# Tying the order of TensorE through a dilated attention mixer, and of VectorE's weight sums ahead of it

## The chip, the cores and the metric

The kernel runs on one core of a Trainium2 chip. The metric is the device time of one execution in microseconds (us); the kernel before has a median of 1405.3 us over three runs (1405.26 to 1405.36). In what follows PE is TensorE, DVE is VectorE, ACT is ScalarE, POOL is GpSimd and SP is SyncE.

## The reference, cut to what matters

A two-layer encoder over 512 tokens of width 1024, all in float32. Each layer is a token mixer and a squared-ReLU MLP, each with a norm ahead and a residual sum behind. The change lies in the first mixer, dilated attention with three head groups g, whose outputs are merged by their softmax denominators:

```python
qkv = (h @ w_qkv).reshape(B, S, 3, N_GROUPS, A_HEADS, A_HEAD_DIM)
for g, (window, dil) in enumerate(((128, 1), (512, 4), (2048, 16))):
    q = rope(rms_norm(qkv[:, :, 0, g], q_gain[g]), S)
    k = rope(rms_norm(qkv[:, :, 1, g], k_gain[g]), S)
    v = qkv[:, :, 2, g]
    o, lse = dilated_group(q, k, v, window, dil)   # softmax over |i-j| <= window/2, every dil-th key
    ...
wts = softmax(stack(lses, 0), axis=0)
o = sum(wts[g][..., None] * outs[g] for g in range(3))
return o.reshape(B, S, 1024) @ w_o
```

There are 8 heads of 128. The second layer's mixer is a latent attention (mixer B); the change does not touch it, nor the MLPs.

## The kernel before, in words

Each float32 product of the large matrices is made of three matmuls on halves: weights are loaded as `raw` (SP's queue), ACT copies the rounded upper part to `whi` (L158), DVE subtracts it for the lower part `wlo` (L159), and PE adds `whi` x upper, `wlo` x upper and `whi` x lower of the activations (L191). `whi` and `wlo` have rings of 4 buffers, `raw` of 3.

The stages follow each other: the **V phase** makes the values v of all groups, mainly by a scheme with seven block products for eight (function `v_phase`, products at L436, each group's blocks `b11` to `b22` and their sums `bT` and `b3` by `add_block`, L349; DVE splits the weights at L422 and adds or subtracts finished products into `vo` at L455). Then **mixer A**, then MLP, **mixer B** and MLP.

Mixer A goes over four head pairs b and three groups g: twelve projection blocks `(b, g)`, each `block_groups` (L163) with four out tiles r of 128 tokens by 512 columns and four weight units u, loaded in two groups of two. So a block has 16 steps `(r, u)`, each of 6 matmuls: steps 0 to 7 take units 0 and 1 for r = 0 to 3, steps 8 to 15 units 2 and 3. The four out tiles take the four PSUM banks of `acc_p`. `qk_evac` empties a bank: ACT squares it (L138, four times), DVE multiplies it with the rotary tables (L288, and L291 twice), makes `rs_v` (L130), POOL raises it to -1/2, DVE adds and scales (L296, L297), ACT rearranges halves (L299), SP's queue transposes by DMA and ACT writes `qkT` (L307).

`scores` (L591, L595 for g = 0, L602 for g = 1 and 2) multiplies q with k into a bank of `sc_p` (two banks), DVE adds a mask, takes a maximum (L598, L607, L610), ACT takes exponentials (L613). `merge` combines the three groups' maxima and denominators through two small matmuls (`scm`, L657 and L682) and DVE scales the probabilities P (L688). `pv` transposes P on PE into a bank of `tp_p` (two banks; L125), copies it (`pT`, on DVE at L698 for groups 1 and 2, on ACT at L705 for group 0) and adds up four heads' products into `sco` (L712, L716), which DVE copies to `oT` (L718). `split_o` (L761, L762) halves `oT` for the out projection `a_w_o`; `v_last` is the value projection of the eighth head, 4 tiles of 384 columns.

[...] The code can add an order of its own: `tc.issue_after(x)` holds what is issued inside behind the instruction x, and (new in the change) `tc.keep_in_program_order` keeps an engine's instructions in the order of the code. In the kernel before, PE's order through mixer A is the scheduler's.

Of the kernel before, what the change touches and what calls it, by code (L numbers as in the profile page):

```python
# [10 lines left out]
F32 = mybir.dt.float32  # L11
# [77 lines left out]
def encoder_kernel(ctx: ExitStack, tc: tile.TileContext, x, norm_mix, norm_ffn, a_w_qkv, a_q_gain, a_k_gain,  # L89
# [33 lines left out]

    def transpose(o, i):
        return PE.transpose(o, i, ident)  # L125
# [36 lines left out]
    def block_groups(units, groups, n, mm, outs=NT, halves=1, raws=None, order=None, between={}, by_k=False):  # L162
# [4 lines left out]
        kt0 = 0  # L167
        for gi, g in enumerate(groups):
# [9 lines left out]
            if by_k and gi == len(groups) - 1:  # L178
                steps = [(*step[:3], [j]) for j in range(loaded[0][2]) for step in steps]
            left = {o: sum(step[1] == o for step in steps) for o in range(outs)}  # L180
            cut = None
            for i, (hv, o, u, js) in enumerate(steps):
                hi, lo, nk = loaded[u]
                with ExitStack() as behind:
                    if cut is not None:
                        behind.enter_context(tc.issue_after(cut))
                        cut = None
                    for j in js:
                        kt = first[u] + j
                        for p_i, (lt, rt, oc) in enumerate(mm(o, kt, hi[:, j], lo[:, j], hv)):  # L190
                            last = PE.matmul(accs[o][:, oc], lhsT=lt, rhs=rt, start=(kt == 0 and p_i == 0 and hv == 0),  # L191
                                             stop=(kt == total - 1 and p_i == 2), skip_group_check=halves > 1)
                if i in between:
                    with tc.issue_after(last.ins):
                        cut = between[i]()
                left[o] -= 1
                if gi == len(groups) - 1 and not left[o]:
                    yield o, accs[o]
            if gi < len(groups) - 1:
                yield None  # L200
# [109 lines left out]
    def qk_proj(b, g, qkT, homes, junk, turned, midway):  # L310

        for end in block_groups(qk_units(b, g), [2, 2], 512, act_stationary(hT, 512)):
            if end is None:
                midway()
            else:
                qk_evac(g, qkT, *end, homes, junk, turned)()

# [4 lines left out]
    def v_phase(vp):  # L322
# [23 lines left out]
        def add_block(t, x, y):  # L346
            for u in range(2):
                us = slice(2 * u, 2 * u + 2)
                V.tensor_tensor(t[:, us], x[:, us], y[:, us], op=ALU.add)  # L349
# [68 lines left out]
        def split_w(x):  # L418
# [3 lines left out]
            V.tensor_tensor(lo, x, hi.bitcast(F32), op=ALU.subtract)  # L422
# [16 lines left out]
        def both(p, w, banks, first):  # L439
            for u, t in ((0, 0), (0, 1), (1, 0), (1, 1)):  # L440
# [21 lines left out]
        def piece(g, ba):  # L462
# [4 lines left out]
            add_block(bT[g], bT[g], b22[g])  # L467
# [66 lines left out]
        for g in range(1, NG):  # L534
# [7 lines left out]
            both(2, b21[g], bd, True)  # L542
            put(g, 0, 0, "set", bd, False)
# [15 lines left out]
    with tc.tile_pool(name="apool", bufs=1, reuse_waits="tile") as ap_, \  # L559
# [19 lines left out]
        def scores(b, g, qkT, Pt, stats):  # L579

            m, den, nb = stats
            for h in range(2):
                qT, kT = qkT[:, h], qkT[:, 2 + h]
                for part in range(2 if g == 0 else 1):
                    sc = sc_p.tile([P, 512], F32, tag="sc", name=nm("sc"))
                    pt = Pt[g][h]
                    if g == 0:
                        for ii in range(2):
                            i = 2 * part + ii
                            q_i = qT[:, i * P:(i + 1) * P]  # L590
                            PE.matmul(sc[:, ii * 256:ii * 256 + 128], lhsT=q_i, rhs=kT[:, i * P:(i + 1) * P],  # L591
                                      start=True, stop=True)
                            segs = bass.AP(tensor=kT.tensor, offset=kT.offset + SEG_A[i],
                                           ap=[list(kT.ap[0]), [SEG_B[i] - SEG_A[i], 2], [1, 64]])
                            PE.matmul(sc[:, ii * 256 + 128:ii * 256 + 256], lhsT=q_i, rhs=segs, start=True, stop=True)  # L595
                        sv = sc.rearrange("p (i k) -> p i k", i=2)
                        pv = pt[:, 2 * part:2 * part + 2, :]
                        V.tensor_tensor(pv, sv, m0[:, 2 * part:2 * part + 2, :], op=ALU.add)  # L598
                        cols = range(2 * part, 2 * part + 2)
                    else:  # L600
                        for r in range(NT):
                            PE.matmul(sc[:, r * P:(r + 1) * P], lhsT=qT[:, r * P:(r + 1) * P],  # L602
                                      rhs=kT[:, r * P:(r + 1) * P], start=True, stop=True)
                        sv = sc.rearrange("p (i k) -> p i k", i=NT)
                        pv = pt
                        mk = (m1 if g == 1 else m2).unsqueeze(1).broadcast_to([P, NT, P])
                        V.tensor_tensor(pv, sv, mk, op=ALU.add)  # L607
                        cols = range(NT)
                    c0, c1 = cols[0], cols[-1] + 1
                    V.tensor_reduce(m[:, g, h, c0:c1], pv, axis=AX.X, op=ALU.max)  # L610
                    V.tensor_scalar(nb[:, g, h, c0:c1], m[:, g, h, c0:c1], -SCALE_A, None, op0=ALU.mult)
                    for c in cols:
                        A.activation(pt[:, c], pt[:, c], AF.Exp, bias=nb[:, g, h, c:c + 1], scale=SCALE_A,  # L613
                                     accum_out=den[:, g, h, c:c + 1])
# [8 lines left out]
        def v_last(vt, v0n, v0c):  # L623
# [7 lines left out]
            run_block(v_units(HA - 1), [1] * 4, 384, act_stationary(hT, 384), evac)  # L631
# [15 lines left out]
        def merge(stats, Pt):  # L647

            m, den, _ = stats
# [6 lines left out]
            for s_ in range(4):  # L656
                PE.matmul(ps[:, 4 * s_:4 * s_ + 4], lhsT=xs[:, s_], rhs=r4, start=True, stop=True)  # L657
# [22 lines left out]
            ps2 = sc_p.tile([P, 512], F32, tag="sc", name=nm("scm"))  # L680
            for h in range(2):
                PE.matmul(ps2[:, 4 * h:4 * h + 4], lhsT=xs2[:, h], rhs=i4, start=True, stop=True)  # L682
            V.tensor_copy(e[:, 0], ps2[:, 0:8])
            ev = e.rearrange("p g (h i) -> p g h i", h=2)
            for h in range(2):
                for g in (1, 2, 0):
                    t = Pt[g][h]
                    V.tensor_tensor(t, t, ev[:, g, h].unsqueeze(2).broadcast_to(list(t.shape)), op=ALU.mult)  # L688

        def pv(b, h, Pt, vt, v0n, v0c):  # L690
            pts = []
            hs = slice(DH * h, DH * h + DH)
            for g in (1, 2):
                tp = tp_p.tile([P, 512], F32, tag="tp", name=nm("tp"))
                for r in range(NT):
                    transpose(tp[:, r * P:(r + 1) * P], Pt[g][h][:, r])
                pT = aw.tile([P, 512], F32, tag="pT", name=nm("pT"), bufs=4)
                V.tensor_copy(pT, tp)  # L698
                pts.append(pT)
            for part in range(2):  # L700
                tp = tp_p.tile([P, 512], F32, tag="tp", name=nm("tp"))
                for i in range(NT):
                    transpose(tp[:, i * P:(i + 1) * P], Pt[0][h][:, i, part * P:(part + 1) * P])
                pT = aw.tile([P, 512], F32, tag="pT", name=nm("pT"), bufs=4)
                A.activation(pT.rearrange("p (i r j) -> p i r j", i=NT, r=NT),  # L705
                             tp.rearrange("p (i j r) -> p i r j", i=NT, r=NT), AF.Copy)
                pts.append(pT)
            o = sc_p.tile([P, 512], F32, tag="sc", name=nm("sco"))
            ov = o.rearrange("p (r m) -> p r m", r=NT)
            for r in range(NT):  # L710
                for g in (1, 2):
                    PE.matmul(o[:, r * P:(r + 1) * P], lhsT=vt[:, r, g - 1, hs], rhs=pts[g - 1][:, r * P:(r + 1) * P],  # L712
                              start=(r == 0 and g == 1), stop=False, skip_group_check=True)
            for i in range(NT):
                for part, vv in ((0, v0n), (1, v0c)):
                    PE.matmul(ov[:, :, 32 * i:32 * i + 32], lhsT=vv[:, i, hs], rhs=pts[2 + part][:, i * P:(i + 1) * P],  # L716
                              start=False, stop=(i == NT - 1 and part == 1), skip_group_check=True)
            V.tensor_copy(oT[:, 2 * b + h], o)  # L718
# [10 lines left out]
        def project_in(b, g, midway=lambda: None):  # L729
            if b == 0 and g:  # L730
                tables(g, gqk[:, g - 1], ca[:, 0:256], ca[:, 256:768])
            qkT = aw.tile([P, 4, S], F32, tag="qkT", name=nm("qkT"))
            qk_proj(b, g, qkT, homes, junk, turned, midway)
            return qkT

        def finish(b, Pt, stats, vs):
            merge(stats, Pt)
            for h in range(2):
# [520 lines left out]
```

## Time and profile before

| | us |
|---|---|
| median of three runs | 1405.3 |
| profiled execution | 1403.76 |
| span of its trace | 1402.0 |
| PE busy | 1371.6 (98%) |
| DVE busy | 940.0 (67%) |
| ACT busy | 801.0 (57%) |
| POOL busy | 224.0 (16%) |

The stages lie about so in the span: V phase to 122 us, mixer A from there to 510, MLP to 830, mixer B to 1040, out projection and MLP to the end. A row of a list of groups gives line, engine, operation, output and inputs, the shape, the count, busy time and mean in ns, and the idle time ahead of it with what ended it. A row of waits gives the engine's line, what ended the wait, the total, the count and the longest. A timeline row gives start, duration, engine, line and operands, and in brackets the idle time ahead. A matmul's end is modelled, so its pace is read from two starts.

### The profile page before, as it was taken

To read this page: it belongs to the slowest core of one execution; us is meant where nothing else is said; L and a number is where in the kernel's file an instruction comes from. 1 tells how busy PE (TensorE), PEld (TensorE's weight loads), DVE (VectorE), ACT (ScalarE), POOL (GpSimd) and SP (SyncE) were. 2 spreads that over 40 slices of the span, in tenths; PEclk is the share of its full clock that TensorE was granted. 3 is DMA by queue.
4 is the path that set the end of the run, shared out by engine and by line. 5 is a ranking of instruction groups with operands and counts; after the bars stand their busy time and mean duration, and the time that the engine had idled before them with its cause. 6 is when DMAs were issued, how large, how long until landed. Compare 5 with 4: busy or idle time off the path is not lost.

```text
span 1402.0 us, 18979 instructions
## 1 busy us (share of the span) xinstructions
PE 1371.6 (98%) x6852; PEld 1163.6 (83%) x6852; DVE 940.0 (67%) x1498; ACT 801.0 (57%) x1643; POOL 224.0 (16%) x240
## 2 busy tenths in 40 slices
PE   7999999999999999999999999999999999999998
PEld 6999887888889989888888878777769888888887
DVE  6886777787788744464655768788745465574747
ACT  6544778687786624453536455777534553644543
POOL 1110212121122001020200204433201020020101
PEclk9999999999999999999999999999999999999999
DMA  9535553655555539486583944211116668493835
GB/s 309 170 134 163 134 130 97 164 131 125 143 130 120 158 106 271 135 186 174 123 237 87 234 96 95 61 31 31 46 46 189 172 131 230 98 234 119 198 88 120
DMA packets 171774, 197.83 MB, mean 141 GB/s; under 512 B 59104, under 2 KB 109024, under 8 KB 171680
## 3 DMA queue, kind: packets, MB, share of 16 engines
q1 hardware_dynamic: 152496, 157.55, 37.7%
q0 software_dynamic: 19184, 39.07, 15.5%
q8 instruction: 54, 0.88, 0.3%
q14 instruction: 40, 0.33, 0.1%
HBM read 176.13 MB, written 7.86 MB: 131 GB/s over the span
## 4 chain that ended last, share of the span: by engine, by line
PE 80%; DVE 7%; DMA 4%; issue 4%; ACT 3%; POOL 1%; SPq 0%; ACTq 0%; DVEq 0%; POOLq 0%
PE acc L191 49%; PE sc L877 9%; PE tp L877 6%; PE sc L436 3%; PE tp L125 2%; DMA wqs<-in_ffn_w_dram 2%; PE acc L1170 1%; DVE wlo L820 1%; PE sc L1064 1%; DMA xT<-t 1%; PE acc L1146 1%; PE tp L436 1%; PE sc L602 1%; PE sco L716 1%; PE sco L712 1%
## 5 line engine op out<-in xcount | busy, mean ns | idle before, releaser
L191 PE MATMUL acc<-whi,hT 128*128 128x512 f32 (+2 forms) x1208 | 377.2, 388 | 1.9 <-ACT hT L761 1.0
L191 PE MATMUL acc<-hT_f,whi 128*128 128x512 f32 (+1 forms) x1152 | 317.5, 366 | 0.0
L159 DVE TENSOR_TENSOR wlo<-raw,whi 128x1024 fp32r<-128x1024 f32 (+3 forms) x146 | 172.8, 1188 | 169.3 <-ACT whi L158 168.8
L191 PEld LDWEIGHTS acc<-whi,hT 128*128 128x128 f32 x1208 | 224.4, 188 | 42.7 <-ACT hT L761 1.7
L158 ACT ACTIVATE whi<-raw 128x1024 fp32r<-128x1024 f32 (+3 forms) x146 | 149.7, 1029 | 159.6 <-PE acc L191 74.8
L191 PEld LDWEIGHTS acc<-hT_f,whi 128*128 128x128 f32 x1152 | 207.9, 189 | 34.9
L191 PE MATMUL acc<-wlo,hT 128*128 128x512 f32 (+2 forms) x604 | 232.9, 386 | 0.4 <-DVE wlo L159 0.4
L820 DVE TENSOR_TENSOR wlo<-wqs,whi 128x1024 fp32r<-128x1024 f32 x112 | 137.7, 1231 | 114.0 <-ACT whi L819 113.9
L819 ACT ACTIVATE whi<-wqs 128x1024 fp32r<-128x1024 f32 x112 | 118.3, 1060 | 162.0 <-PE acc L191 66.2
L191 PE MATMUL acc<-hT_f,wlo 128*128 128x512 f32 (+1 forms) x576 | 204.1, 366 | 0.0
L877 PE MATMUL sc<-whi,asp 128*128 128x512 f32 x512 | 165.1, 390 | 1.0 <-DVE resid L851 1.0
L805 POOL DMA_DIRECT2D wqs<-in_ffn_w_dram x64 | 77.7, 1347 | 539.7 <-DVE wlo L820 358.1
L191 PEld LDWEIGHTS acc<-wlo,hT 128*128 128x128 f32 x604 | 113.7, 188 | 20.1 <-DVE wlo L159 1.0
L191 PEld LDWEIGHTS acc<-hT_f,wlo 128*128 128x128 f32 x576 | 108.3, 189 | 17.3
L877 PEld LDWEIGHTS sc<-whi,asp 128*128 128x128 f32 x512 | 96.2, 188 | 21.6 <-issue 1.8
L877 PE MATMUL tp<-whi,asp 128*128 128x512 f32 x352 | 112.1, 390 | 0.9 <-DVE resid L851 0.9
L133 POOL TENSOR_TENSOR qrs<-rs_v,nhalf 128x4 f32<-128x4 f32 x48 | 64.6, 1348 | 265.0 <-DVE rs_v L130 241.8
L877 PE MATMUL sc<-wlo,asp 128*128 128x512 f32 x256 | 99.7, 390 | 0.0
L307 ACT ACTIVATE qkT<-xT 128x1024 uint16<-128x1024 uint16 x48 | 56.5, 1181 | 39.5 <-DMA xT<-t 39.4
L877 PEld LDWEIGHTS tp<-whi,asp 128*128 128x128 f32 x352 | 66.1, 188 | 15.0 <-DVE resid L851 1.3
L877 PE MATMUL tp<-wlo,asp 128*128 128x512 f32 x176 | 68.2, 390 | 0.0
L138 ACT ACTIVATE junk<-acc 128x128 f32<-128x128 f32 x192 | 52.3, 273 | 12.3 <-PE acc L191 8.7
(236 smaller groups left out, 2186.8 us busy)
## 6 DMA issues: line engine op xcount, KB each, us to landing
wqs<-in_ffn_w_dram SPq DMA_DIRECT2D x80, 512.0 KB, 5.0
raw<-in_ffn_w_dram SPq DMA_DIRECT2D x64, 512.0 KB, 4.6
wqs<-in_ffn_w_dram POOLq DMA_DIRECT2D x64, 512.0 KB, 7.2
raw<-in_a_w_qkv_dram SPq DMA_DIRECT2D x96, 256.0 KB, 3.2
b<-in_a_w_qkv_dram SPq DMA_DIRECT2D x24, 384.0 KB, 5.7
vall<-vo POOLq DMA_DIRECT2D x24, 192.0 KB, 2.3
raw<-in_a_w_o_dram SPq DMA_DIRECT2D x8, 512.0 KB, 4.1
raw<-in_b_w_o_dram SPq DMA_DIRECT2D x8, 512.0 KB, 3.8
```

The source lines that it names most:

```text
L125: return PE.transpose(o, i, ident)
L133: G.tensor_tensor(out, v[:, :n], nhalf[:, :n], op=ALU.pow)
L138: A.activation(junk, x, AF.Square, scale=1.0 / math.sqrt(dim), accum_out=out)
L158: A.activation(hi[:, :nk, :n], raw[:, :nk, :n], AF.Copy)
L159: V.tensor_tensor(lo[:, :nk, :n], raw[:, :nk, :n], hi[:, :nk, :n].bitcast(F32), op=ALU.subtract)
L191: last = PE.matmul(accs[o][:, oc], lhsT=lt, rhs=rt, start=(kt == 0 and p_i == 0 and hv == 0), stop=(kt == total - 1 and p_i == 2), skip_gr ...
L307: A.activation(dst, xT.rearrange("p (h c) t -> p c t h", h=2), AF.Copy)
L436: PE.matmul(banks[t][:, :VH], lhsT=lt, rhs=rt[:, j], start=(first and k == 0 and i_ == 0), stop=(k == 3 and i_ == 2), skip_group_check=True)
L805: marks["sum"] = nc.gpsimd.dma_start(t, src, accum_op=ALU.add).ins
L819: A.activation(hi, x, AF.Copy)
L820: V.tensor_tensor(lo, x, hi.bitcast(F32), op=ALU.subtract)
L877: PE.matmul(bk[t], lhsT=lt, rhs=rt[:, j], start=(first and k == 0 and i_ == 0), stop=(k == 3 and i_ == 2), skip_group_check=True)
```

## The change

Three things are new.

**PE's order through mixer A is tied.** While `tied[0]` holds, every matmul and transpose of PE keeps the order of the code. The code is written so that a projection block runs step by step, whole steps of six matmuls, and the pieces of attention have places behind numbered steps (`sides`): the score parts of the head pair, the merge in two parts (`fold`: first the small matmuls and the scaling of groups 1 and 2, then the second small matmuls and the scaling of group 0), and the four parts of `pv` for each head (transposes of groups 1 and 2, their products, transposes of group 0, their products). The attention of pair c runs in the blocks of pair c+1; that of the last pair runs between the steps of `v_last` and of the first half of the out projection, which now runs in half steps (one k tile after the other over its four out tiles) and lies wholly in the tied stretch.

**DVE's sums in the V phase are tied later.** For groups 1 and 2 the sum `bT` = `b11` + `b12` stands behind the last product subtracted for the group before (`marks["minus"]`) and behind the split of product 2; the sum `b3` stands behind the sum `bT` + `b22`. Products 6 and 7 of these groups finish one out tile before the other. The rotary tables of group 0 move from group 1 to the end of the phase.

**The helpers are split up** so that each piece can be called by itself; what they compute is the same.

On DVE in the V phase, between group 1 (`bT_671`) and group 2 (`bT_949` before, `bT_945` now): in the order before,

```order
L422 TENSOR_TENSOR wlo_866<-b_110_824,whi_865 128x2x384
L349 TENSOR_TENSOR bT_949<-b_124_940,b_125_943 128x768 x2
L422 TENSOR_TENSOR wlo_882<-b_110_824,whi_881 128x2x384
L422 TENSOR_TENSOR wlo_902<-bT_671,whi_901 128x2x384
L455 TENSOR_TENSOR vo<-vo,sc_674 128x384
L349 TENSOR_TENSOR b_150_1098<-b_125_943,b_126_946 128x768
L455 TENSOR_TENSOR vo<-vo,sc_675 128x384
L349 TENSOR_TENSOR b_150_1098<-b_125_943,b_126_946 128x768
L422 TENSOR_TENSOR wlo_918<-bT_671,whi_917 128x2x384
L455 TENSOR_TENSOR vo<-vo,sc_674 128x384
```

and now

```order
L436 TENSOR_TENSOR wlo_862<-b_110_820,whi_861 128x2x384
L436 TENSOR_TENSOR wlo_872<-b_110_820,whi_871 128x2x384
L436 TENSOR_TENSOR wlo_898<-bT_671,whi_897 128x2x384
L469 TENSOR_TENSOR vo<-vo,sc_674 128x384
L469 TENSOR_TENSOR vo<-vo,sc_675 128x384
L436 TENSOR_TENSOR wlo_914<-bT_671,whi_913 128x2x384
L469 TENSOR_TENSOR vo<-vo,sc_674 128x384
L436 TENSOR_TENSOR wlo_951<-b_123_933,whi_950 128x2x384
L469 TENSOR_TENSOR vo<-vo,sc_675 128x384
L436 TENSOR_TENSOR wlo_967<-b_123_933,whi_966 128x2x384
L362 TENSOR_TENSOR bT_945<-b_124_936,b_125_939 128x768 x2
```

The sum for group 2 and the two halves of `b_150` (its `b3`) stood among the splits and vo rows of group 1; the sum now stands behind the last of these vo rows.

On DVE at the second part of a merge (here the second head pair's, whose place is in block (2,1)), where `me` is the weight of group 0, `P` 128x1024 a scaling of group 0, and `pT` the copies of the first head's transposes: before,

```order
L683 COPY me_3090<-scm_3103 128x8
L698 COPY pT_3118<-tp_3113 128x512
L159 TENSOR_TENSOR wlo_3521<-raw_3517,whi_3520 128x1024
L698 COPY pT_3125<-tp_3120 128x512
L297 TENSOR_TENSOR t_601_3367<-t_601_3367,qrs_3374 128x512
L296 TENSOR_TENSOR t_608_3400<-t_608_3400,t_609_3401 128x512
L688 TENSOR_TENSOR P_2329<-P_2329,me_3090 128x1024
L688 TENSOR_TENSOR P_2330<-P_2330,me_3090 128x1024
```

and now

```order
L711 COPY me_3132<-scm_3233 128x8
L308 TENSOR_TENSOR t_566_3206<-t_566_3206,t_567_3207 128x512
L669 TENSOR_TENSOR P_2620<-P_2620,me_3132 128x1024
L669 TENSOR_TENSOR P_2667<-P_2667,me_3132 128x1024
L727 COPY pT_3244<-tp_3239 128x512
L300 TENSOR_TENSOR t_578_3259<-acc_3080,cosg_1228 128x512
L727 COPY pT_3251<-tp_3246 128x512
```

The two copies stood ahead of the scalings of group 0 and now stand behind them. The third pair's rows read the same; in the first pair one copy stands right behind `me`, the other behind the scalings.

On DVE at the end of the projections, where `acc_4385` before and `acc_4242` now are the last out tile of block (3,2), whose bank the fourth tile of `v_last` takes next: before,

```order
L598 TENSOR_TENSOR P_4081<-sc_4114,ca 128x512
L610 TENSOR_REDUCE stat_4087<-P_4081 128x2
L288 TENSOR_TENSOR t_848_4579<-acc_4385,cosg_1230 128x512
L291 TENSOR_TENSOR t_849_4580<-acc_4385,sing_1231 128x4x64 x2
L130 TENSOR_SCALAR rs_v_4584<-qss_4573 128x4
```

and now

```order
L625 TENSOR_TENSOR P_4607<-sc_4606,ca 128x512
L300 TENSOR_TENSOR t_844_4564<-acc_4242,cosg_1230 128x512
L138 TENSOR_SCALAR rs_v_4569<-qss_4558 128x4
L308 TENSOR_TENSOR t_835_4518<-t_835_4518,t_836_4519 128x512
L628 TENSOR_REDUCE stat_4368<-P_4607 128x4
L303 TENSOR_TENSOR t_845_4565<-acc_4242,sing_1231 128x4x64 x2
```

The pair L291 (now L303), the bank's last reader, stood right behind the first reader and now stands behind `rs_v`, another tile's sum and a reduction. On PE the fourth tile of `v_last` starts one score and three steps behind the end of block (3,2); before, the scheduler ran three tiles of `v_last` with a first, one with a second weight unit and some scores ahead of the fourth tile.

The core of the diff:

```diff
+    def on_pe(ins):
+        return tc.keep_in_program_order(ins) if tied[0] else ins
+
+    def multiply(out, **kw):
+        return on_pe(PE.matmul(out, **kw))
...
-            if by_k and gi == len(groups) - 1:
+            if by_k == "all":
+                steps = [(0, o, u, [j]) for u in range(g) for j in range(loaded[u][2]) for o in range(outs)]
+            elif by_k and gi == len(groups) - 1:
...
-                if i in between:
+                if at + i in between:
                     with tc.issue_after(last.ins):
-                        cut = between[i]()
+                        cut = between[at + i]()
...
-        def both(p, w, banks, first):
-            for u, t in ((0, 0), (0, 1), (1, 0), (1, 1)):
+        def both(p, w, banks, first, by_tile=False):
+            for u, t in ((0, 0), (1, 0), (0, 1), (1, 1)) if by_tile else ((0, 0), (0, 1), (1, 0), (1, 1)):
...
             b3 = vp.tile([P, 4, VH], F32, tag="h32", name=nm("b3"))
-            add_block(b3, b12[g], b22[g])
-            both(6, bT[g], ba, False)
+            with ExitStack() as behind:
+                if g:
+                    behind.enter_context(tc.issue_after(after_t))
+                add_block(b3, b12[g], b22[g])
+            both(6, bT[g], ba, False, g > 0)
             put(g, 0, 1, "sub", ba, True)
-            add_block(bT[g], bT[g], b21[g])
-            both(7, b3, ba, False)
+            marks["sums", g] = add_block(bT[g], bT[g], b21[g])
+            both(7, b3, ba, False, g > 0)
             put(g, 1, 1, "sub", ba, True)
+            marks["minus", g] = marks["put"]
...
-            if g == 1:
-
-                with tc.issue_after(marks["put"]):
-                    tables(0, g0, rot[:, 0:256], rot[:, 256:768])
-            add_block(bT[g], b11[g], b12[g])
+            with tc.issue_after(marks["minus", g - 1]), tc.issue_after(seconds):
+                add_block(bT[g], b11[g], b12[g])
             piece(g, ba)
+        with tc.issue_after(marks["sums", NG - 1]):
+            tables(0, g0, rot[:, 0:256], rot[:, 256:768])
...
+        def fold(b, i):
+            if i == 0:
+                folds[b] = merge(stats[b], Pt[b])
+                return
+            folds[b]()
+            pvs[b] = [pv(b, h, Pt[b], *vs[b]) for h in range(2)]
...
+        def sides(b, g):
+
+            if b == 0:
+                return [{}, {13: at((score, 0, 0, 0)), 15: at((score, 0, 0, 1))},
+                        {1: at((score, 0, 0, 2)), 3: at((score, 0, 0, 3)), 14: at((score, 0, 1, 0))}][g]
+            c = b - 1
+            return [{0: at((score, c, 1, 1)), 13: at((score, c, 2, 0)), 15: at((score, c, 2, 1))},
+                    {3: at((fold, c, 0)), 11: at((fold, c, 1), (part, c, 0, 0)), 13: at((part, c, 0, 1)),
+                     14: at((part, c, 0, 2))},
+                    {0: at((part, c, 0, 3)), 1: at((part, c, 1, 0)), 3: at((part, c, 1, 2)), 4: at((part, c, 1, 1)),
+                     5: at((part, c, 1, 3)), 6: at((score, b, 0, 0)), 7: at((score, b, 0, 1)),
+                     8: at((score, b, 0, 2), (score, b, 0, 3)), 14: at((score, b, 1, 0))}][g]
+
+        tied[0] = True
         for b in range(HA // 2):
...
-        merge(stats, Pt)
-        v_last(*vs)
+        c = HA // 2 - 1
+        v_last(*vs[c], {1: at((score, c, 1, 1)), 12: at((score, c, 2, 0)), 13: at((score, c, 2, 1)),
+                        15: at((fold, c, 0))})
...
-        pv(HA // 2 - 1, 0, Pt, *vs)
-        first_cols = block_groups(w_units(a_w_o[0], 0, 512), [3, 1], 512, act_stationary(oA, 512, {0: o0}), by_k=True)
-        next(first_cols)
-        pv(HA // 2 - 1, 1, Pt, *vs)
-        for h in (HA - 2, HA - 1):
-            split_o(h)
+        first_cols = block_groups(w_units(a_w_o[0], 0, 512), [3, 1], 512, act_stationary(oA, 512, {0: o0}), by_k="all",
+                                  between={12: at((fold, c, 1), (part, c, 0, 0)), 15: at((part, c, 0, 1)),
+                                           17: at((part, c, 0, 2)), 19: at((part, c, 1, 0)),
+                                           20: at((part, c, 0, 3), (split_o, HA - 2)),
+                                           22: at((part, c, 1, 1), (part, c, 1, 2)),
+                                           24: at((part, c, 1, 3), (split_o, HA - 1))})
+        first_cols = iter([*first_cols])
+        tied[0] = False
```

`part(c, h, i)` calls the i-th of the four pieces of `pv` for head h of pair c: 0 turns groups 1 and 2 (`turn_strided`), 1 adds their products (`add_strided`), 2 turns group 0 (`turn_near`), 3 adds its products (`add_near`).

More of the change, by code (lines that the diff above doesn't have):

```diff
@@ L308, in qk_evac, with qk_proj @@
         return end
[L310 to L315, printed above, removed]
+    def qk_proj(b, g, home, homes, junk, turned, between):
+        qkT = None
+        for end in block_groups(qk_units(b, g), [2, 2], 512, act_stationary(hT, 512), between=between):
+            if end is not None:
+                qkT = qkT or home()
                 qk_evac(g, qkT, *end, homes, junk, turned)()
+        return qkT
     def load_gains(g, gqk):
@@ L348, in add_block @@
                 us = slice(2 * u, 2 * u + 2)
[L349 removed]
+                last = V.tensor_tensor(t[:, us], x[:, us], y[:, us], op=ALU.add)
+            return last.ins
         def load_x(r):
@@ L577, in encoder_kernel, with scores @@
         sel, r4, sel2, i4 = cc(C_SEL, C_R4), cc(C_R4, C_SEL2), cc(C_SEL2, C_I4), cc(C_I4, C_ALL)
-        def scores(b, g, qkT, Pt, stats):
+        def scores(g, h, part, qkT, Pt, stats):
             m, den, nb = stats
[L582 to L614, printed above, removed]
@@ L679, in merge, with rest @@
                                 sel2.unsqueeze(2).broadcast_to([P, 32, NT]), op=ALU.mult)
[L680 to L683, printed above, removed]
             ev = e.rearrange("p g (h i) -> p g h i", h=2)
             for h in range(2):
-                for g in (1, 2, 0):
-                    t = Pt[g][h]
-                    V.tensor_tensor(t, t, ev[:, g, h].unsqueeze(2).broadcast_to(list(t.shape)), op=ALU.mult)
+                for g in (1, 2):
+                    scale(g, h)
+            def rest():
+                ps2 = sc_p.tile([P, 512], F32, tag="sc", name=nm("scm"))
+                for h in range(2):
+                    multiply(ps2[:, 4 * h:4 * h + 4], lhsT=xs2[:, h], rhs=i4, start=True, stop=True)
+                V.tensor_copy(e[:, 0], ps2[:, 0:8])
+                for h in range(2):
+                    scale(0, h)
+            return rest
         def pv(b, h, Pt, vt, v0n, v0c):
@@ L708, in pv @@
[L708 to L717, printed above, removed]
@@ new lines, in add_near @@
+            def add_near():
+                ov = o[0].rearrange("p (r m) -> p r m", r=NT)
+                for i in range(NT):
+                    for part, vv in ((0, v0n), (1, v0c)):
+                        multiply(ov[:, :, 32 * i:32 * i + 32], lhsT=vv[:, i, hs],
+                                 rhs=pts[2 + part][:, i * P:(i + 1) * P],
+                                 start=False, stop=(i == NT - 1 and part == 1), skip_group_check=True)
+                V.tensor_copy(oT[:, 2 * b + h], o[0])
@@ L727, in turned, with project_in @@
             return aw.tile([P, 8, P], U16, tag="xT", name=nm("xT"))
-        def project_in(b, g, midway=lambda: None):
+        qk, Pt, stats, vs, folds, pvs = {}, {}, {}, {}, {}, {}
+        def project_in(b, g, between):
             if b == 0 and g:
                 tables(g, gqk[:, g - 1], ca[:, 0:256], ca[:, 256:768])
[L732 to L736, printed above, removed]
-            merge(stats, Pt)
-            for h in range(2):
-                pv(b, h, Pt, *vs)
@@ L742, in encoder_kernel, with score @@
-        qkT = project_in(0, 0)
+            qk[b, g] = qk_proj(b, g, lambda: aw.tile([P, 4, S], F32, tag="qkT", name=nm("qkT")), homes, junk,
+                               turned, between)
+        def score(b, g, i):
+            if (g, i) == (0, 0):
+                vs[b] = v_load(b)
+                Pt[b] = [{}, {}, {}]
+                stats[b] = [st.tile([P, NG, 2, NT], F32, tag=f"stat{j}", name=nm("stat"), bufs=2) for j in range(3)]
+            scores(g, i // 2 if g == 0 else i, i % 2, qk[b, g], Pt[b], stats[b])
```

115 lines of the change are left out of this document (80 added, 35 removed).

## The prediction

> **What bounds the kernel now.** I read the page's first part, then the busy time by window (a stretch, its length, the busy time of PE, its weight loads, DVE, ACT and POOL, the granted clock, the DMA share and GB/s), then the list of what TensorE waited for, then the timeline at the waits.
>
> ```profile
> span 1402.0 us, 18979 instructions
> PE 1371.6 (98%) x6852; PEld 1163.6 (83%) x6852; DVE 940.0 (67%) x1498; ACT 801.0 (57%) x1643; POOL 224.0 (16%) x240
> ```
>
> ```profile
> 0.00:20.00 20.00, 10.51 (x49) 9.25 (x50) 10.31 (x16) 12.65 (x22) 1.98 (x8) 1.00 0.96 295
> ...
> 260.00:340.00 80.00, 78.53 (x421) 67.35 (x420) 63.58 (x130) 63.50 (x184) 14.92 (x12) 1.00 0.53 135
> ```
>
> TensorE (PE) is the bound: 1371.6 of 1402.0 us. In a steady stretch of mixer A (260 to 340) PE idles 1.47 us and VectorE (DVE) and ScalarE (ACT) are 79% busy. So an order can win only PE's waits in the stages that it touches, and these are few (who waited for whom, us in total, times, longest):
>
> ```profile
> PE tp L125 <- DVE xn L376: 8.9, 1, 8.9
> PE sco L716 <- ACT pT L705: 1.5, 1, 1.5
> PE sc L436 <- DVE vo L455: 1.0, 3, 0.6
> PE acc L191 <- ACT hT L761: 1.0, 1, 1.0
> PE sc L436 <- DVE wlo L422: 0.6, 1, 0.6
> PE tp L125 <- ACT pT L705: 0.5, 1, 0.5
> PE sc L602 <- ACT qkT L307: 0.5, 2, 0.3
> PE acc L191 <- DVE wlo L159: 0.4, 1, 0.4
> PE tp L125 <- DVE P L688: 0.4, 1, 0.4
> ```
>
> The 8.9 us stand at the kernel's start, which the change leaves alone. The two L436 rows are the V phase: 1.6 us in 4 waits. The other six rows are mixer A: 4.3 us in 7 waits, 1.5 of them in two waits at its end (hT L761 and the transposes behind pT). These idle times count from the modelled end of the matmul before, so what a wait costs is read from starts:
>
> ```profile
> 84.66 0.34 PE L436 MATMUL sc<-whi,Ssp 128*128 128x384 f32 x1
> 85.63 0.41 PE L436 MATMUL sc<-whi,Ssp 128*128 128x384 f32 x1 [0.62 <-DVE vo L455]
> 85.88 0.34 PE L436 MATMUL sc<-wlo,Ssp 128*128 128x384 f32 x1
> 86.05 0.51 PE L436 MATMUL sc<-whi,Ssp 128*128 128x384 f32 x2
> ...
> 263.53 1.95 PE L712 MATMUL sco<-pT,vt 128*128 128x128 f32 x16
> 265.32 0.39 PE L591 MATMUL sc<-qkT 128*128 128x128 f32 x2
> ...
> 299.62 0.61 PE L191 MATMUL acc<-whi,hT 128*128 128x512 f32 x2
> ...
> 302.35 0.60 PE L602 MATMUL sc<-qkT 128*128 128x128 f32 x4
> ```
>
> A 384-column matmul is followed by the next after 0.17 us (85.88 to 86.05), but the one at 84.66 by 85.63: 0.97, so that wait cost 0.80 where its row says 0.62. The modelled end of the matmul ahead (0.34) overhangs its pace (0.17). I add 0.17 to each of the 11 waits: 5.9 + 11 x 0.17 = **7.8 us is what the change can win** (V phase 2.3, mixer A 5.5, of that 1.8 at its end). Twelve 512-column matmuls take 2.73 us (299.62 to 302.35): a step of six is 1.36. Sixteen 128-column records take 1.79 (263.53 to 265.32), 0.11 each, and one fp32 product is two records, 0.22.
>
> **The change, part by part.** PE's instructions keep their number and shapes: none is added or removed, so the rest of the sum is waits.
>
> *V phase.* The sum for the next group is made on DVE at 81.46, among the splits and vo rows, and PE's wait for vo is at 85.63; behind the last product subtracted for the group before DVE stood idle for 2.88 us, ahead of the row at 65.12:
>
> ```profile
> 65.12 0.96 DVE L422 TENSOR_TENSOR wlo<-b,whi 128x768 fp32r<-128x768 f32 x1 [2.88 <-ACT whi L421]
> ...
> 81.46 1.82 DVE L349 TENSOR_TENSOR bT<-b,b 128x768 f32<-128x768 f32 x2
> 83.20 0.95 DVE L422 TENSOR_TENSOR wlo<-b,whi 128x768 fp32r<-128x768 f32 x1
> ```
>
> A pair of sums holds DVE 1.74 us (81.46 to 83.20). Tied behind the last "minus" of the group before, it falls into a gap of 2.88 us (up to 65.12), which hides it; without this cover it would cost at most its own 1.74 twice. All four waits are shorter than 1.74, so I take them as gone: **-2.3** (bounds 0 and -2.3). The tables, moved to the end of the phase, have no reader there.
>
> *Mixer A, per head pair.* The five waits inside (2.8 + 5 x 0.17 = 3.7) come from matmuls that stood just behind what they read. The places keep one to three steps of projections (1.4 to 4.1 us) between: **-3.7**. But one place comes too early, the same for three head pairs. Behind step 11 of block (b,1) stand the second merge matmuls and the first transposes; two steps later add_strided reads both pT. In DVE's new order the copies pT stand behind the two 1024-wide scalings of P. The prices:
>
> ```profile
> 301.61 1.23 DVE L159 TENSOR_TENSOR wlo<-raw,whi 128x1024 fp32r<-128x1024 f32 x1 [1.05 <-ACT whi L158]
> 302.75 0.68 DVE L288 TENSOR_TENSOR t<-acc,cosg 128x512 f32<-128x512 f32 x1
> 303.35 0.74 DVE L291 TENSOR_TENSOR t<-acc,sing 128x256 f32<-128x256 f32 x2
> 304.01 0.16 DVE L130 TENSOR_SCALAR rs_v<-qss 128x4 f32<-128x4 f32 x1
> ...
> L688 DVE TENSOR_TENSOR P<-P,me 128x1024 f32<-128x1024 f32 x8 | 9.4, 1212 | 0.0
> ```
>
> So 1024 elements hold DVE 1.14 us (301.61 to 302.75), 512 hold it 0.60, copies too, the L291 pair 0.66, and a small row, on whose starts nothing waits, some 0.08. Counted from the end of the second merge matmuls, in the second and third pair: about 0.2 to the reader (an estimate: the overhang of 0.17 of PE's last matmul), COPY 0.08, L308 0.60, two scalings 2.28, pT 0.60, L300 0.60, pT 0.68 to its end: 5.04, and some 0.1 back to PE. PE wants the second pT after eight transposes (8 x 0.11), twelve matmuls (2.73) and the first product (0.22): 3.84. It waits 1.3. In the first pair one pT stands ahead, but waits for its four transposes: the second ends at 5.4, a wait of 1.66. Sum 1.66 + 2 x 1.30 = **+4.3**. Bounds: 0, if DVE comes to this place with L308 and L300 behind it and PE late, and 9, if DVE is a further 1.5 late each time. DVE at 79% is nearer to neither.
>
> *The end of mixer A.* The old waits there go: **-1.8**. Two come. In v_last, whose steps are 6 x 0.173 = 1.04, the fourth out tile takes the bank of the last tile of block (3,2), which has then ended 3 x 1.04 + 0.89 (a score) = 4.0 us before. That bank's readers stand behind other work on ACT:
>
> ```profile
> 299.45 1.18 ACT L307 ACTIVATE qkT<-xT 128x1024 uint16<-128x1024 uint16 x1
> 300.52 1.05 ACT L158 ACTIVATE whi<-raw 128x1024 fp32r<-128x1024 f32 x1
> 301.47 0.27 ACT L138 ACTIVATE junk<-acc 128x128 f32<-128x128 f32 x1
> ...
> 302.26 0.28 ACT L138 ACTIVATE junk<-acc 128x128 f32<-128x128 f32 x1
> ```
>
> Four squares at 0.40 (two from 301.47 to 302.26) with a 768-wide whi (three quarters of 0.95), a rearrangement L299 of whi's size (0.95) and a qkT (1.07) between them: 4.3, with 0.2 ahead. Behind that DVE does rs_v, L308, a reduction and the L303 pair: 0.08 + 0.60 + 0.60 + 0.66. Together 6.4, and 0.1 to PE: 6.5 - 4.0 = 2.5. Then the merge: from its first matmuls to its second PE has thirteen half steps of 3 x 0.2275, 8.9 us. The chain between them stands behind six hT rows and two weight splits on both engines: 0.2 + 2.9 (six of 512 columns at half of 0.95) + 0.95 + 0.2 to the exponential, the next whi by 6.6 (its slot comes free at 5.5), wlo 1.14, six small rows 1.3: 9.1, and two scalings more for the transposes: late by 0.7 in all. **+3.2**, bounds 0 and 6.
>
> Sum: 1403.76 - 2.3 - 3.7 - 1.8 + 4.3 + 3.2 = 1403.5 for a profiled execution. The runs' median lies 1.5 above the profiled one (1405.3 against 1403.76), so **1405.0 is forecast**: as many waits come as go.
>
> The row of the first 20 us has a granted clock of 1.00 although an 8.9 us wait lies in it. [...]
>
> **The rivals.**
>
> *The places fit.* If DVE and ACT run ahead of PE where I have them behind, the new waits shrink to a quarter: 7.8 won, 1.9 lost, 1399.4. For it: ACT waits and DVE gaps exist in every stretch, and both engines' work is the same as before. Against: the rows stand in DVE's queue as said, and the first half of the sum (two scalings, 2.28) has no way round.
>
> *The banks come late: slower.* A block's tile r ends with step 9 + 2r and its bank is wanted with step 2r of the next block, six steps or 8.2 us later. Emptying takes 2.9 alone (1.6 of squares, 0.60, 0.66). It decides once more than 5.3 us of other work stands ahead. With PE tied, nothing else can be taken while it waits. At 0.6 us in each of nine handovers with attention between: 1405.0 + 5.4 = 1410.4. For it: 79% busy engines with 1 us rows. Against: no row of the waits names the bank's last reader L291.
>
> *The V phase's ties change nothing*, since other rows stand ahead of the same readers: 1405.0 + 2.3 = 1407.3.
>
> [...]
>
> **How the numbers follow.** A measurement of this kernel tells from no change what is over 0.2%, 2.8 us: faster is below 1402.5, slower above 1408.1. Forecast, with its own range of 1402.5 to 1408: 0.36. V phase without effect 0.06, clock 0.01, both within 0.2% too. Places fit 0.34. Banks late, or the new waits at their upper bounds, 0.23. So faster 0.34, same 0.43, slower 0.23. The range reaches to both neighbours: below to 1398.5 (7.8 won, 1 lost), above to 1410.5.
>
> **What would show it.** In the list of PE's waits: no sc behind vo or wlo (V phase right); three waits of 1.3 to 1.7 of the first L130 product of sco on DVE's pT (the too early place right), absent if the places fit; one of about 2.5 in v_last behind L303 and some tenths of scm and tp behind DVE at the merge. Waits of acc on DVE L303 in many blocks would show the banks. Wrong is the forecast if PE's idle time between 20 and 520 us falls below 3 us or rises above 9.

## The result, and the profile after

The changed kernel takes 1421.1 us (median of four runs, 1420.0 to 1422.2) against 1405.3: a ratio of 1.0112, 95% interval 1.0094 to 1.0129. It is 15.7 us slower; 1405.0 was forecast, with a range that ended at 1410.5. The profiled execution took 1420.1 us, its span is 1418.3.

The page's first rows and the list of PE's waits in the stretch 20 to 560 us, which holds the V phase and mixer A:

```profile
span 1418.3 us, 18969 instructions
PE 1377.0 (97%) x6852; PEld 1166.8 (82%) x6852; DVE 943.9 (67%) x1498; ACT 803.8 (57%) x1643; POOL 219.8 (15%) x240
```

```profile
PE sco L130 <- DVE pT L727: 5.7, 4, 2.9
PE acc L130 <- DVE rs_v L138: 4.6, 4, 2.2
PE acc L130 <- DVE t L303: 4.5, 3, 2.4
PE sc L450 <- DVE vo L469: 1.3, 2, 0.6
PE tp L133 <- DVE P L669: 0.2, 1, 0.2
```

The old waits of mixer A (for qkT, wlo, hT, pT on ACT) are all gone, and three new rows stand there with 14.8 us: products of a head for the copies pT, and projections for a bank. A wait for `rs_v` or L303 is a wait for the bank whose last reader is L303; `rs_v` is the row behind it. In the V phase two of four waits are gone. Together the rows make 16.3 us of idle time; more than 9 was named as a sign that the forecast is wrong. Mixer A by one window of each kernel (before, then after; the second window is 12 us longer, mixer A some 16):

```profile
130.00:510.00 380.00, 375.61 (x2011) 323.04 (x2010) 282.00 (x560) 274.37 (x765) 64.61 (x48) 1.00 0.53 138
```

```profile
130.00:522.00 392.00, 376.61 (x1994) 321.80 (x1993) 282.75 (x557) 275.92 (x764) 60.35 (x48) 0.99 0.51 133
```

PE's idle time there grows from 4.4 to 15.4 us, and the granted clock falls from 1.00 to 0.99. Added up over all neighbouring matmuls, as the distance of their starts less 0.227, 0.173 or 0.11, PE loses some 16 us more in mixer A (24.7 where it lost 8.4 before; the two sums move by up to 3 us with what is taken as the pace of the shortest matmuls, their difference by less than 1), 2.0 in the V phase where it lost 3.2 (-1.2), and 1.0 more in the first 20 us; the later stages differ by 0.2 in all. That makes about 16 us, and the spans differ by 16.3.

**The copies.** DVE's timeline at the first merge, and PE's at the products that wait for it:

```profile
240.15 0.69 DVE L300 TENSOR_TENSOR t<-acc,cosg 128x512 f32<-128x512 f32 x1 [0.43 <-ACT junk L146]
...
241.49 0.16 DVE L711 COPY me<-scm 128x8 f32<-128x8 f32 x1
241.56 0.68 DVE L727 COPY pT<-tp 128x512 f32<-128x512 f32 x1
242.16 0.68 DVE L308 TENSOR_TENSOR t<-t,t 128x512 f32<-128x512 f32 x1
242.76 2.35 DVE L669 TENSOR_TENSOR P<-P,me 128x1024 f32<-128x1024 f32 x2
245.03 0.68 DVE L300 TENSOR_TENSOR t<-acc,cosg 128x512 f32<-128x512 f32 x1
245.63 0.68 DVE L727 COPY pT<-tp 128x512 f32<-128x512 f32 x1
```

```profile
243.10 0.38 PE L130 MATMUL sco<-pT,vt 128*128 128x128 f32 x2
246.36 3.36 PE L130 MATMUL sco<-pT,vt 128*128 128x128 f32 x14 [2.88 <-DVE pT L727]
249.37 0.61 PE L130 MATMUL acc<-whi,hT 128*128 128x512 f32 x1
```

The rows run as forecast, the second copy behind two scalings. But DVE reached `me` at 241.49, 2.1 us behind the end of the merge matmuls (the transposes behind them start at 239.43) where 0.2 was forecast: a tile's three rows ahead (L300, L303 and rs_v) had to be done first, and they began late, behind ACT's squares (`junk`).

**The banks.** The queues of ACT, DVE and PE at the fourth tile of block (1,0), which takes the bank that is last read at 205.17 (the third tile's, with the same names, is last read at 200.00):

```profile
202.31 1.18 ACT L319 ACTIVATE qkT<-xT 128x1024 uint16<-128x1024 uint16 x1
203.38 0.40 ACT L631 ACTIVATE P<-P,stat 128x128 f32<-128x128 f32 x1
...
204.16 0.28 ACT L146 ACTIVATE junk<-acc 128x128 f32<-128x128 f32 x1
```

```profile
197.00 0.68 DVE L300 TENSOR_TENSOR t<-acc,cosg 128x512 f32<-128x512 f32 x1
...
200.00 0.75 DVE L303 TENSOR_TENSOR t<-acc,sing 128x256 f32<-128x256 f32 x2
...
204.56 0.69 DVE L300 TENSOR_TENSOR t<-acc,cosg 128x512 f32<-128x512 f32 x1
205.17 0.74 DVE L303 TENSOR_TENSOR t<-acc,sing 128x256 f32<-128x256 f32 x2
```

```profile
203.47 0.39 PE L130 MATMUL acc<-whi,hT 128*128 128x512 f32 x1
206.06 0.47 PE L130 MATMUL acc<-whi,hT 128*128 128x512 f32 x1 [2.20 <-DVE rs_v L138]
```

The bank's four squares are strewn among exponentials and qkT rows of ACT, L300 starts only behind the fourth, and PE, which wanted the bank at 203.7, goes on at 206.06. For the third tile's bank 2.4 us of other rows lie between its two readers (197.60 to 200.00). Of the 7 waits for banks, five lie in the blocks, all at a fourth tile, and two in v_last, at its third and its fourth.

### The profile page after: what moved, and what is told of

It reads as the page before. It is cut to its first block, busy times and chain, and to the rows that moved or that the text cites. A ratio compares the mean times of both kernels' runs of the same rounds, so it can differ in the third digit from the quotient of the medians.

```text
span 1418.3 us, 18969 instructions
## 1 busy us (share of the span) xinstructions
PE 1377.0 (97%) x6852; PEld 1166.8 (82%) x6852; DVE 943.9 (67%) x1498; ACT 803.8 (57%) x1643; POOL 219.8 (15%) x240
## 3 DMA queue, kind: packets, MB, share of 16 engines
q0 software_dynamic: 19184, 39.07, 15.4%
## 4 chain that ended last, share of the span: by engine, by line
PE 58%; DVE 4%; ACT 2%; issue 1%; POOL 0%; DMA 0%; DVEq 0%; ACTq 0%; POOLq 0%
PE acc L130 31%; PE sc L938 11%; PE tp L938 7%; PE tp L133 2%; PE acc L1231 1%; PE sc L1125 1%; PE acc L1207 1%; DVE wlo L881 1%; PE sc L1207 1%; DVE resid L912 1%; PE acc L133 1%; PE tp L1231 1%; PE sco L130 1%; DVE asp L843 0%; DVE S L874 0%
## 5 line engine op out<-in xcount | busy, mean ns | idle before, releaser
L130 PE MATMUL acc<-whi,hT 128*128 128x512 f32 (+2 forms) x1208 | 388.9, 391 | 10.2 <-DVE rs_v L138 4.6
L141 POOL TENSOR_TENSOR qrs<-rs_v,nhalf 128x4 f32<-128x4 f32 x48 | 60.4, 1261 | 285.5 <-DVE rs_v L138 232.0
L311 ACT ACTIVATE t<-t 128x1024 uint16<-128x1024 uint16 x48 | 50.3, 1053 | 19.1 <-DVE t L309 19.1
```

What stands on the lines that cost most here:

```text
L130: return on_pe(PE.matmul(out, **kw))
L141: G.tensor_tensor(out, v[:, :n], nhalf[:, :n], op=ALU.pow)
L311: A.activation(halves.rearrange("p (h n) -> p h n", h=2), t1.rearrange("p c d -> p (c d)").bitcast(U16).rearrange("p (n h) -> p h n", h=2) ...
```

## The experiments

Each row of a wait below is from the list of PE's waits of the kernel named. Ratios are to the kernel before on the same chip, with 95% intervals.

### The parts of the change

One kernel is the kernel before with all edits of the change to the V phase and none to mixer A:

```diff
-            add_block(bT[g], b11[g], b12[g])
+            with tc.issue_after(marks["minus", g - 1]), tc.issue_after(seconds):
+                add_block(bT[g], b11[g], b12[g])
...
```

> The kernel before with only the V phase of the change (sums tied later, products 6 and 7 by out tile, tables at the end); mixer A as before. Theory: all of the loss comes from mixer A, and the V phase gains what its waits show, 3.2 us of excess between 20 and 125 us before against 2.0 after: 1404.1, within 0.6. Rival (the V phase hands a worse start to mixer A): 1407 or more.

It took 1409.9 us, 1.0038 (1.0023 to 1.0053): 5 us slower, so the theory fell as a forecast of the time. PE lost 2.0 us in the V phase, as in the change, so the gain of 1.2 there is real. But in mixer A, whose code is that of before, it lost 16.9 instead of 8.4 (in the profiled execution, the slowest of four with 1412.0 us). Part of that is pace: from 493 to 500 us the granted clock was 0.64. The two longest rows of waits there:

```profile
PE sc L607 <- ACT qkT L307: 2.2, 4, 1.1
PE tp L125 <- DVE P L693: 2.0, 1, 2.0
```

These waits are not those of before, and PE's, DVE's and ACT's orders through mixer A are others too. Why the framework's scheduler orders mixer A anew behind an edit ahead of it, no run shows.

The reverse, mixer A as in the change and the whole V phase as before:

```diff
-            with tc.issue_after(marks["minus", g - 1]), tc.issue_after(seconds):
-                add_block(bT[g], b11[g], b12[g])
+            add_block(bT[g], b11[g], b12[g])
...
```

> The change with the V phase of before, so mixer A's tied order alone. Theory (in the kernel before, the V phase's change cost 5 us only because the scheduler ordered mixer A anew behind it; where PE's order is tied that cannot happen): 1420 to 1424, the V phase's 1.2 us lost again. Rival (the V phase's change delays the start of mixer A by itself): 1414 to 1418.

1422.4 us, 1.0120 (1.0104 to 1.0135), as the theory had it: 1.3 us above the change, which fits the V phase's own 1.2 but is no more than runs of one kernel differ (1420.0 to 1422.2 for the change). Where PE's order is tied, no loss of 6 us follows from the V phase in mixer A. So the whole loss arises in mixer A.

The tie taken out:

```diff
-        tied[0] = True
```

> The change with the tie alone left out: the code, its places and the V phase are the same, but PE's order through mixer A is the scheduler's again. Theory (the loss is PE standing at a bank or a copy while other matmuls could run): 1402 to 1408. Rival (the new pieces and places cost the time whatever the order): 1415 or more.

1415.1 us, 1.0072 (1.0057 to 1.0087), just inside the rival's range: of 16 us the tie itself costs 6, with the new orders that DVE and ACT get without it. With the same pieces and places, PE's order by the scheduler has few waits for banks, and others instead, most of them for the copies `pT` (6.7 us for DVE's, 2.3 for ACT's).

### The copies behind the scalings

```diff
-                    {3: at((fold, c, 0)), 11: at((fold, c, 1), (part, c, 0, 0)), 13: ...
+                    {3: at((fold, c, 0)), 11: at((part, c, 0, 0), (fold, c, 1)), 13: ...
...
```

> The change with one edit: at step 11 the first head's transposes and the copies of them stand ahead of the second merge matmuls and of group 0's scaling. Theory (the copies behind two scalings make the three waits of sco for pT, 3.0 + 2.4 + 1.1 us, and the first of them the slow stretch of 1.5 us behind it): 7 to 8 us less, 1413 to 1414. Rival (DVE is late there anyway): less than 3 us less, 1418 or more.

1413.9 us, 1.0064 (1.0049 to 1.0079), 7 us less than the change. The copies then stand ahead of the scalings in DVE's queue, and of the 5.7 us of sco for pT 0.2 are left, while 1.1 came new for transposes behind pT and the waits for banks are nearly as they were (8.6 us for 9.1):

```profile
PE acc L130 <- DVE rs_v L138: 4.3, 4, 2.2
PE acc L130 <- DVE t L303: 4.3, 3, 2.2
...
PE tp L133 <- DVE pT L727: 1.1, 1, 1.1
...
PE sco L130 <- DVE pT L727: 0.2, 1, 0.2
```

The theory had the first merge's slow stretch, 1.5 us, go as well. That one is gone, but in v_last the granted clock is now 0.50 and 0.53 over six microseconds (465 to 471), so what slow stretches cost did not fall. The profiled execution is the slowest of four, 1414.9, and lies 5 us below the change's.

### What holds the banks

First an order by hand: a tile's sum, scaling and rearrangement stand behind the next tile's squares and table products, and a score's rows behind those of the last tile.

```diff
-                qk_evac(g, qkT, *end, homes, junk, turned)()
+                nxt = qk_evac(g, qkT, *end, homes, junk, turned)
+                if turn:
+                    behind_banks(turn)
+                turn = nxt
```

(`behind_banks` calls its function with `issue_after` on the last square and the last L303; a score is called through it too.)

> The change with one edit at the emptying of a bank: the sum, scaling and rearrangement of an out tile stand behind the next tile's squares and table products, and a score's rows on ACT and DVE behind those of the tile emptied last, so that the rows that free a bank stand together. Theory (banks come late because these rows are spread among others in ACT's and DVE's queues): the waits of acc in the blocks (5.5 us) and in v_last (4.0 us and 1.5 us of slow stretch) shrink by half or more, 1411 to 1416. Rival (ACT and DVE have too much to do there, in any order): waits move to other rows, 1418 or more.

1460.9 us, 1.0394 (1.0377 to 1.0412): the waits did not move, they grew fourfold, and the mean granted clock fell to 0.984 (the change: 0.997). The group of L303 on DVE says why; before, after, and in this kernel, with the idle time ahead of the group at the end; the last fence is the wait that grew:

```profile
L291 DVE TENSOR_TENSOR t<-acc,sing 128x256 f32<-128x256 f32 x96 | 36.0, 414 | 13.3 <-DMA xT<-t 13.2
```

```profile
L303 DVE TENSOR_TENSOR t<-acc,sing 128x256 f32<-128x256 f32 x96 | 35.9, 416 | 11.0 <-DMA xT<-t 10.9
```

```profile
L303 DVE TENSOR_TENSOR t<-acc,sing 128x256 f32<-128x256 f32 x96 | 36.0, 416 | 37.3 <-DMA xT<-t 37.3
```

```profile
PE acc L130 <- DVE t L303: 36.6, 14, 5.4
```

L303 writes `t2`, of which there are two buffers, and a buffer comes free when the DMA transpose has read it, at the end of a chain through DVE, POOL, DVE, ACT and the queue. So the bank's release hangs on the whole evacuation of the tile two before, and putting that evacuation later, as this kernel does, makes the bank later. The row of before already shows it. The next kernel is the change with a third buffer:

```diff
-            return [aw.tile([P, 4, DH], F32, tag=t, name=nm(t)) for t in ("t1", "t2")]
+            return [aw.tile([P, 4, DH], F32, tag=t, name=nm(t), bufs=n) for t, n in (("t1", 2), ("t2", 3))]
```

> The change with one size different: three buffers instead of two for t2, which the last reader of a bank (L303) writes and which comes free only when the DMA transpose of two tiles before has read it. Theory (L303, and with it the bank, waits for that ring, so DVE's order puts it behind other rows): the waits of acc in the blocks and in v_last (9.1 us by their rows) at least halve, with less slow stretch behind them, 1409 to 1416. Rival (the squares' places in ACT's queue hold the banks): 1418 or more.

1408.7 us, 1.0025 (1.0016 to 1.0034), 12 us less than the change. L303 never waits, and where 2.4 us of other rows lay between the two readers they now follow each other; PE's waits for these banks fall from 9.1 to 3.7 (3.4 and 0.3 for L303), and one of 0.8 is new, for a bank that v_last fills and ACT copies (`vt`). These rows are of the fastest of ten executions, 1405.6. The group, the timeline at the third tile of block (1,0) and the waits:

```profile
L303 DVE TENSOR_TENSOR t<-acc,sing 128x256 f32<-128x256 f32 x96 | 36.0, 415 | 0.0
```

```profile
194.11 0.68 DVE L300 TENSOR_TENSOR t<-acc,cosg 128x512 f32<-128x512 f32 x1
194.71 0.75 DVE L303 TENSOR_TENSOR t<-acc,sing 128x256 f32<-128x256 f32 x2
```

```profile
PE acc L130 <- DVE rs_v L138: 3.4, 2, 2.1
...
PE sco L130 <- DVE pT L727: 1.1, 2, 0.7
PE acc L130 <- ACT vt L648: 0.8, 1, 0.8
```

The wait for the copies shrinks too, from 5.7 to 1.1, though DVE comes to the merge no earlier: it reaches `me` 2 to 3 us behind the merge matmuls in each of the three pairs (238.89 in the first, whose transposes start at 235.90). The edit changes one size, but the scheduler orders DVE and ACT anew for it, and in all three pairs both copies now stand ahead of the scalings, as in the kernel that puts the copies first. So the 12 us are not the ring's alone. Against that kernel, whose copies stand so too, the third buffer is worth 5 us (1413.9 to 1408.7), part of it pace: the mean granted clock of the profiled execution is 0.999 here and 0.997 there (0.94 there from 420 to 480 us). What is left of the banks (1.2 us at the block and 2.1 in v_last) is a wait for `rs_v`, behind the squares.

The same edit in the kernel before:

> The kernel before with three t2 buffers and nothing else. Theory (there no wait of PE names the bank's last reader, so the ring costs nothing): no gain; but the scheduler orders mixer A anew, which may cost some us: 1403 to 1412. Rival (the ring held back PE in the kernel before too): 1402 or less.

1411.8 us, 1.0048 (1.0031 to 1.0064). L291's idle time of 13.3 us is gone there too (0.0), and nothing is won: the ring did not hold PE in that order, and the scheduler's new order cost 7 us, as the theory allowed.

### The end of mixer A, and combinations

v_last in pairs of weight units, so that the fourth tile's bank is wanted three steps later:

```diff
-            run_block(v_units(HA - 1), [1] * 4, 384, ...
+            run_block(v_units(HA - 1), [2, 2], 384, ...
```

> The change with one edit: v_last loads its weight units two by two, so that it works unit by unit pair on one out tile after the other and wants the fourth tile's bank behind six steps and a score (7.1 us) and not behind three (4.0). Theory (the banks of the last two tiles of block (3,2), given back late, cost 4.0 us there and 1.5 of slow stretch behind): 4 to 6 us less than the change, 1415 to 1417. Rival (what is gained there is waited for later, at the merge): 1419 or more.

1417.7 us, 1.0094 (1.0076 to 1.0112), between the two expectations. The two waits for banks at the end fell from 1.3 and 2.4 to 0.4 and 1.0, and 1.2 came back as a score's wait for qkT: part of the gain is given back, as the rival had it.

The copies first, three `t2` buffers and no tie from v_last on (`tied[0] = False` ahead of it):

> The change with three edits: three t2 buffers, the first head's copies ahead of the scaling of group 0, and no tie from v_last on. Theory (the three causes add up: 7 from the copies, 5 to 10 from the banks, 3 to 5 from the end): 1400 to 1406. Rival (another order brings its own waits, as the other kernels showed): 1408 or more.

1404.8 us, 0.9996 (0.9987 to 1.0005). With the three edits the whole loss is gone; it is not faster than before. The parts overlap and do not simply add up: alone the copies gave 7 us and the third buffer 12, more than the 16 lost, since the order that came with the third buffer puts the copies first too. Taking the tie away from v_last on was not tried alone.

The same with the tie to the end and v_last in pairs:

> The change with three t2 buffers, the first head's copies ahead of the scaling of group 0, and v_last in pairs of units; PE tied to the end. Theory (the three causes are separate; with three t2 buffers alone the copies still cost 1.6 and v_last 2.7): 1402 to 1405. Rival (the order brings new waits): 1407 or more.

1407.5 us, 1.0020 (1.0011 to 1.0030), in the rival's range: the waits for banks are 0.9, but scores in v_last wait 3.0 for qkT, which the late banks had covered. And with places moved besides:

```diff
-            return [{0: at((score, c, 1, 1)), 13: ...
+            return [{4: at((score, c, 1, 1)), 13: ...
-                    {..., 11: at((part, c, 0, 0), (fold, c, 1)), 13: at((part, c, 0, 1)), 14: at((part, c, 0, 2))},
+                    {..., 12: at((part, c, 0, 0), (fold, c, 1)), 14: at((part, c, 0, 1)), 15: at((part, c, 0, 2))},
-                    ... 3: at((part, c, 1, 2)), 4: at((part, c, 1, 1)),
+                    ... 4: at((part, c, 1, 2), (part, c, 1, 1)),
...
```

> As the kernel with v_last in pairs, three t2 buffers and the copies first, with places moved besides: the second score of group 1 behind step 4 and not 0 of block (b,0) (its rows stand ahead of the squares of the last tile of the block before) and behind step 5 of v_last, the second part of the merge and the first head's parts one step later, the second head's products together. Theory (the wait for the bank at the fourth tile of block (1,0), 1.4 us, and waits at the merge of 0.7 go): 1400 to 1403. Rival (moving places moves waits): 1405 or more.

1422.9 us, 1.0122 (1.0104 to 1.0140), against a theory of 1400 to 1403. The wait for the bank in block (1,0) stayed (2.1 us), so the score's place was not its cause, and products of group 0, now one step behind their transposes, waited for pT:

```profile
PE sco L130 <- ACT pT L744: 5.6, 6, 2.0
PE sco L130 <- DVE pT L727: 4.9, 5, 2.3
```

The mean granted clock of that execution is 0.993, against 0.999 without the moved places, so pace has a part in these 15 us too.

No kernel tried beats the one before. What delays the squares of the fourth tile of block (1,0) was not tried apart.

## Why the prediction was wrong, point by point

**The old waits go:** right. All seven in mixer A are gone (5.5 us). In the V phase two of four are left, so 1.2 us were won and not 2.3. The sums no longer stand ahead of vo, as forecast, but ahead of the two waits that are left stands the split of a weight (`wlo`), which had itself waited for ACT.

**The too early place:** the mechanism was right, and the experiment that puts the copies first shows it. Its size was 4.3 and is 5.7 by the waits' rows, with 0.17 for each of the four 6.4. The term that was mis-sized is DVE's start: 0.2 us behind the merge matmuls in the sum, 2.1, 1.5 and 0.2 in the three pairs. The 0.1 back to PE stood on no row; from the second copy's end to the product behind it, the change has 0.05 to 0.06 in the three pairs (246.31 to 246.36 in the first).

**The end of mixer A:** the wait at the fourth tile of v_last was forecast at 2.5 and is 2.55 from start to start, but that is luck. Its bank came free 8.2 us behind the end of block (3,2) (463.03 to 471.22) and not 6.5, and PE wanted it after 5.6 and not 4.0, because the third tile's wait of 1.5, which was not foreseen, had held PE up: two errors of the same size. The merge's wait was 0.7 and is 0.6.

**The banks:** this is the step that failed. In the sum the banks of the blocks stood at nothing, because "Emptying takes 2.9 alone" and 8.2 us are there for it; late banks were only a rival with a price of 5.4, which shared a chance of 0.23 with the new waits at their upper bounds. Banks cost 9.1 us by the rows and with 0.17 for each of seven waits 10.3, of which 2.5 were in the sum: 7.8 us were not. The rival's mechanism was right, its number was not: an emptying is not 2.9 us and what stands ahead, it also hangs on the buffer that L303 writes. With a third buffer the waits fall to 3.7, and with the evacuations put later they rise to 36.6. "No row of the waits names the bank's last reader L291" was read as evidence against; it said only that in the scheduler's order PE had other matmuls to do meanwhile. The row of L291 with 13.2 us of waiting for the transposes was in the profile of before and was not read.

**The clock:** the weighing was wrong. Its chance of 0.01 rests on no run; beside it stood only the row of the first 20 us, which shows a granted clock of 1.00 over the wait of 8.9 us. The pace behind that wait, in the timeline of before, shows the opposite:

```profile
13.35 0.84 PE L436 MATMUL acc<-whi,hT 128*128 128x384 f32 x2
13.98 0.52 PE L436 MATMUL acc<-wlo,hT 128*128 128x384 f32 x1
...
14.75 0.34 PE L436 MATMUL acc<-wlo,hT 128*128 128x384 f32 x1
14.92 0.34 PE L436 MATMUL acc<-whi,hT 128*128 128x384 f32 x1
```

From 13.35 to 13.98 two matmuls take 0.63, 0.32 each, with no idle time marked ahead, and behind 14.75 0.17 each. In the changed kernel two waits are followed by such a stretch, and there the window shows it:

```profile
246.00:249.00 3.00, 2.64 (x12) 2.64 (x13) 2.77 (x8) 1.06 (x1) 1.81 (x2) 0.54 0.00 0
...
471.00:474.00 3.00, 2.78 (x10) 2.81 (x11) 2.04 (x5) 2.79 (x9) 0.00 (x0) 0.59 0.09 25
```

Fourteen records take 3.0 us (246.36 to 249.37) and not 1.5, and in v_last ten matmuls 0.15 more each: 3.0 us in the two, which no term held. The first stretch stands behind one wait of 2.9 us, the second behind two of 1.3 and 2.4 with 1.1 us of work between; no run varied the length of these waits by itself.

**The account.** By the waits' rows, in mixer A new waits are 15.0 us (the three rows and one of 0.2 for P), 17.0 with 0.17 for each of the twelve, slow stretches 3.0, old waits -5.5: 14.5 of 16.3. The other 1.8 lie in distances below 0.2 us each and were not followed up. The forecast had 7.5 for the new waits and nothing for the clock.

## What to carry to other kernels

Before tying an engine's order, price a buffer's release by the whole chain that ends it: the bank here was held by a ring of two scratch buffers that a DMA frees. One more buffer (2 KB a partition) gave back 12 of 16 us, some 5 of them beyond what an order with the copies first gives. That no wait names a resource in a kernel whose order a scheduler chose does not mean that the resource has slack; look at what its readers themselves wait for (here 13.2 us of L291 for the transposes). And where a scheduler orders everything, an edit in one stage can cost more in the next than it wins: 1.2 us won and 6 lost.

## What was not expected of the hardware

The same wait does not always bring a slow stretch. In the kernel with v_last in pairs the first merge's wait is again 2.88 us, and behind it the fourteen records run at full pace, 1.6 us instead of 3.0:

```profile
246.01 1.83 PE L130 MATMUL sco<-pT,vt 128*128 128x128 f32 x14 [2.88 <-DVE pT L727]
247.59 0.47 PE L130 MATMUL acc<-whi,hT 128*128 128x512 f32 x1
```

That execution has a mean granted clock of 1.000 and 1415.0 us; the other three of that kernel have 0.997 and 1417.6 to 1419.4. So such a kernel has a spread of some microseconds that one profile doesn't show. Not every spread is the clock's: with three t2 buffers ten executions take 1405.6 to 1411.4, and one with a clock of 1.000 takes 1409.3. What spreads them was not looked into. And the granted clock in a window's row is not to be trusted at the start of the trace, where the row of 11 to 14 us reads 1.00 over matmuls 0.32 us apart, which are 0.17 apart from 14.75 us on.
